# Value products in one run, rows scaled in the addition, attention's half first: one hybrid encoder layer on Trainium2

## The chip, the cores and the metric

The kernel runs on one core of one Trainium2 chip, in one launch. The metric is the device time in microseconds (us); lower is better. The times shown are medians of several runs, and beside them stands one execution taken with the hardware profiler. A core has five engines that run their own instruction streams: TensorE (PE, with its weight loads PEld), VectorE (DVE), ScalarE (ACT), GpSimd (POOL) and SyncE (SP), whose work here is the issue of DMAs.

## The reference

One layer of an encoder on x of 2048 rows by 1024 columns. Cut to what matters here:

```
proj = rms_norm(x, g_mix) @ w_in                      # q 8x64, k 2x64, v 2x64, u 512
attn = window_attention(rope(q), rope(k), v, sink)    # blocks of 128, window +-128, 512 wide
ys   = gelu(s5_bidirectional(u, ...))                 # state space, both directions, 512 wide
ys   = ys * sigmoid(ys @ w_glu)
mixed = concat([rms_norm(attn, g_attn), rms_norm(ys, g_ssm)])
x = x + mixed @ w_out
h = rms_norm(x, g_ffn)
up = depthwise_conv(h @ w_up, conv_w, conv_b)         # width 3
x = x + (silu(up[:, :2816]) * up[:, 2816:]) @ w_down
out = rms_norm(x, g_final)
```

A block of 128 queries sees up to three blocks of keys, its own and its two neighbours (the first and the last block see two). rms_norm divides every row by the root of the mean of its squares (plus a small constant) and multiplies each column by a gain.

## The kernel before

The kernel works in stages. First come the input projection and the tables of the state space part, then the state space part itself (s5), with the projections of q, k and v beside it. Then attention and the stage called join run side by side, and the feed-forward part (ffn) comes last. Products that need full float32 accuracy are made in three passes: a number is split into a high part that TensorE's faster float32 form (F32R) holds exactly and the rest, and `mm3` (lines 73 to 80) multiplies high by high, high by low and low by high into the same PSUM bank.

**Attention** (lines 478 to 630) is a generator. After its setup it takes five steps for each of 32 pairs (block b, key head kv), so ten steps a block. While it weighs the values of one pair it makes the logits and the softmax of the next:

1. `logits` of the next pair, query heads 0 and 1 (sp, line 556, with VectorE's masked maximum at line 557); for kv 0 the loads and splits of the next queries and keys.
2. `turn_p` for key tiles 0 and 1: four transposes each (ptp, line 579) and a copy by ScalarE (ph, line 581).
3. `logits`, heads 2 and 3; then `weigh` of key tile 0.
4. `turn_p` of key tile 2, `weigh` of key tile 1, and the `softmax` of the next pair (lines 559 to 573: exponentials on ScalarE, the division on VectorE).
5. `weigh` of key tile 2, which ends in ScalarE's copy of av into aT; for kv 0 `turn_q` and `turn_k`, transposes of the next queries and keys (ptq, ptk).

`weigh` (lines 584 to 591) multiplies one key tile's values (128 keys by 64) into two halves of the output's partitions, one matmul for each half. They are float32 and the trace has two records for each, so four for a call:

```
for o in (0, 1):
    nc.tensor.matmul(av[64 * o:64 * o + 64], vt[order[ki]][:, kv], ph4[:, o], start=ki == 0, ...)
```

**Join** (lines 632 to 811) is a generator too. For each block b it makes the output projection in two halves of 512 columns (po). Each half is five groups of matmuls, over parts 4 to 7 of the mixed row first (the state space half) and 0 to 3 (attention) after them. Behind each of the first four groups of a half it takes one item of a list called todo and yields; it also yields at the end of each half. That gives ten yields and eight slots to a block. The list has eight items:

- `gate(b + 2)`, three: loads y, transposes it (gpt, line 667), multiplies it by w_glu (pg), applies the gate, and scales the rows by their reciprocal root mean square rs (line 691).
- `turn(b - 1)`, two: transposes the normalised row block hx (gpt<-hx) and stores it, with sums and differences in the second four blocks of each half of the rows, as operands of the feed-forward part (lines 723 to 756). Some of these are made in hx itself and stored from there.
- `halves(b + 1)`, three: squares aT and sums it over the four parts (lines 707, 708); sums over the partitions with a matmul against ones (pr, line 711) and takes the power -1/2 on POOL (`rstd`, line 119), and transposes and splits y into parts 4 to 7; spreads that reciprocal over the columns with a matmul against the identity (pr, line 718), multiplies aT by it on VectorE (line 719) and splits it into parts 0 to 3.

At the end of a block the rows are x + po (line 794); they are stored, squared into hx (line 804), and hx becomes the normalised rows (line 807). There is one hx buffer.

**Order.** `build` advances attention by one step for each of join's yields in the steady part and by 1.5 before it. So a block of join goes with a block of attention, and join is at block b while attention works at b + 2. This is the program's order. The tile framework hands the instructions to the engines when the kernel is built, by a schedule of its own. In the trace PE's order in this stage is nearly the program's, with some instructions later than they are written, such as the transposes of keys among the po that follow. Each engine runs its own list in order and waits at an instruction until what it needs is there. PSUM here has three banks for join (R), one for av (psa), two for sp and two for transposes (pt).

Of the kernel before, what the change touches and what calls it, by code (L numbers as in the profile page):

```python
# [3 lines left out]

# [1 line left out]

# [17 lines left out]
NB = 16  # L24
# [5 lines left out]
EPS = 1e-6  # L30
# [25 lines left out]
class Net:  # L56
# [25 lines left out]
    def setup(self):  # L82
        nc, tc = self.nc, self.tc
        c = self.cpool = self.pool(self.ctx, "const")
        d = self.pool(self.ctx, "scratch", space=DRAM)
        self.ident = c.tile([128, 128], F32, name="ident")
        self.identr = c.tile([128, 128], F32R, name="identr")
        self.mhalf = c.tile([128, 1], F32, name="mhalf")
        nc.vector.memset(self.mhalf, -0.5)
        self.ones = c.tile([128, 1], F32, name="ones")  # L90
        nc.vector.memset(self.ones, 1.0)
        warm = c.tile([128, 1], F32, name="warm")
        nc.scalar.activation(warm, self.ones, AF.Copy)
        self.r16 = c.tile([128, 16, 2], F32, name="r16")
        self.rx = c.tile([128, NB], F32, name="rx")
        self.cw = c.tile([128, 2 * NF, 4], F32, name="cw")
        self.qkv_d = d.tile([L, 768], F32, name="qkv_d")
        self.u_d = d.tile([L, 512], F32, name="u_d")
        self.q_d = d.tile([T, 64, 128], F32, name="q_d")
        self.e_d = d.tile([16, 128, 2, 2, 128], F32, name="e_d")  # L100
        self.kp_d = d.tile([16, 2, 32, 2, 256], F32, name="kp_d")
        self.y_d = d.tile([L, 512], F32, name="y_d")
        self.x1_d = [d.tile([128, D], F32, name=f"x1_{t}") for t in range(NB)]
        self.bop_d = [{m: d.tile([128, 4, HALF], F32, name=f"bo{b}{m}") for m in BOP} for b in (0, 1)]
        self.act_d = [d.tile([2 * n, 128, L], F32, name=f"act{c}") for c, n in enumerate(DN)]
        self.wsum_d = [{m: d.tile([128, n, HALF], F32, name=f"ws{c}{m}") for m in ("t1", "t2", "t3", "t4")} for c, n in enumerate(DN)]
        self.gN = None
        self.st_f = ExitStack()
        self.left = False
# [368 lines left out]
    def attention(self):  # L478
        nc, tc, a = self.nc, self.tc, self.a
        V, S, G = nc.vector, nc.scalar, nc.gpsimd  # L480
        with ExitStack() as st:
# [117 lines left out]
            for n in range(2 * NB):  # L599
                b, kv = divmod(n, 2)  # L600
                nb, nkv = divmod(n + 1, 2)
                nk = len(window(b)[0])
                more, new = nb < NB, kv == 0 and b + 1 < NB
                if more:
                    logits(nb, nkv, (0, 1))
                if new:
                    qs = load_q(b + 1)
                    ks = load_kv(b + 2) if b + 2 < NB else None
                yield
                ph = [turn_p(b, kv, ki) for ki in (0, 1)]  # L610
                yield
                if more:
                    logits(nb, nkv, (2, 3))
                av = self.psa.tile([128, 512], F32, tag="pa", name=self.nm("av"))[:, 0:256]
                weigh(b, kv, av, 0, ph[0])
                yield
                if nk == 3:
                    ph.append(turn_p(b, kv, 2))
                weigh(b, kv, av, 1, ph[1])
                if more:  # L620
                    softmax(nb, nkv)
                yield
                if nk == 3:
                    weigh(b, kv, av, 2, ph[2])
                if new:
                    turn_q(b + 1, qs)
                    if ks is not None:
                        turn_k(b + 2, ks)
                del sms[b, kv]
                yield  # L630

    def join(self):
# [21 lines left out]
            return r  # L654

        def out_piece(n):
            k, c = (n + 4) % 8, n // 8
            r = p.tile([128, 512], F32, tag=("x1", "hx")[n % 3 == 2], name=self.nm("woraw"), bufs=2 - (n % 3 == 2))
            nc.sync.dma_start(r, a["w_out"][128 * k:128 * (k + 1), 512 * c:512 * c + 512])
            h, l, sc = wo[c][0][:, k], wo[c][1][:, k], gas[:, k:k + 1]  # L660
            S.activation(h, r, AF.Copy, scale=sc)
            V.scalar_tensor_tensor(l, r, sc, h.bitcast(F32), ALU.mult, ALU.subtract)
# [7 lines left out]
        def gate(b):  # L670
# [13 lines left out]

            S.activation(sg, pg, AF.Tanh, scale=0.5)
            V.scalar_tensor_tensor(y, sg, 1.0, y, ALU.add, ALU.mult)
            ssq = g.tile([128, 1], F32, tag="gssq", name=self.nm("gssq"))
            S.activation(sg, y, AF.Square, accum_out=ssq)
            rs = g.tile([128, 1], F32, tag="grs", name=self.nm("grs"))
            self.rstd(rs, ssq, 512, g, 4 * EPS)  # L690
            V.tensor_scalar(y, y, rs, None, ALU.mult)
            yield

        def halves(b):

            h = p.tile([128, 8, 128], F32R, tag="oh", name=self.nm("oh"))
            l = p.tile([128, 8, 128], F32R, tag="ol", name=self.nm("ol"))
            split[b] = h, l

            def part(src, k):  # L700
                S.activation(h[:, k:k + 4], src, AF.Copy)
# [4 lines left out]
            sr = p.tile([128, 128], F32, tag="sr", name=self.nm("sr"), bufs=1)  # L706
            S.activation(sq, aT, AF.Square)
            V.tensor_reduce(sr, sq.rearrange("p a q -> p q a"), axis=AX.X, op=ALU.add)
            yield
            pr = self.R.tile([128, 512], F32, tag="x", name=self.nm("pr"))  # L710
            nc.tensor.matmul(pr[:, 0:1], sr, self.ones[:, 0:1])
            ra = p.tile([128, 1], F32, tag="ra", name=self.nm("ra"))
            self.rstd(ra, pr[:, 0:1], 512, p)
            part(trans(ys.pop(b)), 4)
            yield

            pr = self.R.tile([128, 512], F32, tag="x", name=self.nm("pr"))
            nc.tensor.matmul(pr[:, 0:128], ra.to_broadcast([128, 128]), self.ident)
            V.tensor_tensor(aT, aT, bc(pr[:, 0:128], 1, 4), op=ALU.mult)
            part(aT, 0)  # L720
            yield

        def turn(b, hx):
# [48 lines left out]
            yield False  # L772
        hx = None
        for b in range(NB):
            h, l = split.pop(b)
            if b == NB - 2:
                gst.close()
            first = gate(b + 2) if b + 2 < NB else halves(b + 1) if b + 1 < NB else iter([None] * 4)
            todo = chain(first, turn(b - 1, hx) if b else (), halves(b + 1) if b + 2 < NB else ())
            rows = slice(128 * b, 128 * (b + 1))  # L780
            x1 = p.tile([128, D], F32, tag="x1", name=self.nm("x1"))
            nc.sync.dma_start(x1, a["x"][rows, :])
            for c in (0, 1):
                po = self.R.tile([128, 512], F32, tag="x", name=self.nm("po"))
                sl = slice(512 * c, 512 * c + 512)
                for n, ks in enumerate(((4, 5), (6, 7), (0, 1), (2,), (3,))):
                    self.mm3(po, [(h[:, k], l[:, k], wo[c][0][:, k], wo[c][1][:, k]) for k in ks], n == 0, n == 4)
                    for i in (next(late, None), next(late, None)):
                        if i is not None:
                            out_piece(i)  # L790
                    if n < 4:
                        next(todo, None)
                        yield True
                V.tensor_tensor(x1[:, sl], po, x1[:, sl], op=ALU.add)
                if c == 0:
                    if b == NB - 1:
                        wst.close()
# [579 lines left out]
```

## Time and profile before

| | |
|---|---|
| Median of three runs | 2161.92 us (2161.03 to 2167.24) |
| Profiled execution, its own time | 2166.09 us |
| Its span in the trace | 2164.3 us |
| PE busy | 2066.8 us (95%) |
| VectorE busy | 1696.6 us (78%) |
| ScalarE busy | 1054.1 us (49%) |
| POOL busy | 158.6 us (7%) |
| DMA moved | 320.14 MB |

Attention's value products run from 413.3 to 824.5 us in the trace, the output projection's matmuls from 450.5 to 859.5. Busy time is the time that an engine's instructions cover. Matmuls overlap: a matmul of 512 columns lasts about 0.39 us in the records, but the next begins before it ends. So the cost of a matmul in a row of matmuls is read from one start to the next. A line of the timeline gives start, length, engine, source line, operation, what is written from what, the shape, and how many equal instructions in a row it stands for. In brackets stands idle time before it, with what ended that. In a table of stretches the numbers behind an engine are its busy microseconds and, in brackets, its instructions; the granted clock of TensorE, the DMA engines' busy share and GB/s follow.

### The profile page before, as it was taken

The page shows a single profiled execution, that of the slowest core. Times are in us where ns is not written, and L with a number is a line of the kernel's source. Part 1 is how long each engine was busy: PE and PEld are TensorE (multiplying, and loading weights), DVE is VectorE, ACT ScalarE, POOL GpSimd, SP SyncE. Part 2 cuts the span into 40 slices and gives each one's busy share as a digit, 9 for nine tenths or more (in the row PEclk, how much of TensorE's full clock was granted, in tenths as well). Part 3 has the DMA queues.
Part 4 walks back from the last instruction along what each step waited for, and adds up shares of the span by engine and source line. Part 5 has one row for each costly group of instructions (what it writes and reads, how often), then busy time and mean ns, then how long its engine had stood idle before and what let it go on. Part 6 is the DMA issues. An engine that isn't in the chain of part 4 may idle for free.

```text
span 2164.3 us, 27908 instructions
## 1 busy us (share of the span) xinstructions
PE 2066.8 (95%) x10000; PEld 1667.8 (77%) x10000; DVE 1696.6 (78%) x3008; ACT 1054.1 (49%) x1847; POOL 158.6 (7%) x244
## 2 busy tenths in 40 slices
PE   7998889799999999999999999999999999998997
PEld 5787777567777777788888887888888787887886
DVE  8978888675566557788888898898988967756885
ACT  5524444776666654544444454544444634324332
POOL 0400000000000001000000000010100010000111
PEclk9999999899999999999999999999999999999999
DMA  8975655533244228522233363343432567856642
GB/s 280 343 196 153 193 168 168 165 103 93 76 130 122 77 80 258 170 88 82 96 107 125 117 208 109 122 164 119 149 138 86 163 151 196 203 110 182 183 158 88
DMA packets 204043, 320.14 MB, mean 148 GB/s; under 512 B 13312, under 2 KB 134656, under 8 KB 203904
## 3 DMA queue, kind: packets, MB, share of 16 engines
q1 hardware_dynamic: 182160, 245.41, 36.2%
q0 software_dynamic: 18304, 70.26, 11.1%
q10 hardware_dynamic: 3440, 2.69, 0.4%
q8 instruction: 78, 1.28, 0.2%
q14 instruction: 61, 0.50, 0.1%
HBM read 213.98 MB, written 104.33 MB: 147 GB/s over the span
## 4 chain that ended last, share of the span: by engine, by line
PE 68%; issue 10%; DMA 9%; DVE 9%; ACT 3%; POOL 1%; SPq 1%; ACTq 0%; POOLq 0%; DVEq 0%
PE py L1120 19%; PE pz L1120 12%; PE px L1120 12%; PE po L78 3%; PE av L589 2%; PE po L79 2%; PE po L80 2%; PE sp L556 2%; PE ptp L579 2%; DMA kp_d<-kk 2%; PE pp L80 1%; PE pp L79 1%; PE pp L78 1%; PE gpt L667 1%; DMA y_d<-yt 1%
## 5 line engine op out<-in xcount | busy, mean ns | idle before, releaser
L1120 PE MATMUL px<-b,g1h 128*128 128x512 f32 x1056 | 327.1, 391 | 6.1 <-ACT cu L1148 5.0
L1120 PEld LDWEIGHTS px<-b,g1h 128*128 128x128 f32 x1056 | 198.4, 188 | 49.4 <-ACT cu L1148 6.7
L1120 PE MATMUL px<-b,g1l 128*128 128x512 f32 x528 | 206.3, 391 | 1.1 <-DVE g1l L1043 0.9
L1120 PE MATMUL py<-bt,s2h 128*128 128x512 f32 x528 | 166.9, 398 | 4.6 <-ACT s2h L1042 4.6
L1120 PE MATMUL py<-bt,g2h 128*128 128x512 f32 x528 | 164.0, 391 | 3.7 <-DVE cu L1174 3.7
L1120 PE MATMUL py<-bt,s1h 128*128 128x512 f32 x528 | 162.9, 389 | 0.1
L1120 PE MATMUL pz<-bt,s1h 128*128 128x512 f32 x528 | 162.7, 389 | 0.0
L1120 PE MATMUL pz<-b,s4h 128*128 128x512 f32 x528 | 162.6, 389 | 0.0
L1042 ACT ACTIVATE s1h<-st 128x1024 fp32r<-128x1024 f32 (+1 forms) x67 | 69.4, 1036 | 120.8 <-PE py L1120 120.7
L1120 PEld LDWEIGHTS py<-bt,s2h 128*128 128x128 f32 x528 | 101.3, 192 | 26.8 <-ACT s2h L1042 5.8
L1120 PEld LDWEIGHTS py<-bt,g2h 128*128 128x128 f32 x528 | 99.1, 188 | 25.9 <-DVE cu L1174 4.1
L1120 PEld LDWEIGHTS px<-b,g1l 128*128 128x128 f32 x528 | 99.4, 188 | 22.9 <-DVE g1l L1043 2.2
L1120 PEld LDWEIGHTS py<-bt,s1h 128*128 128x128 f32 x528 | 99.1, 188 | 21.1 <-DVE bt L1008 0.5
L1120 PEld LDWEIGHTS pz<-b,s4h 128*128 128x128 f32 x528 | 99.1, 188 | 20.6
L1120 PEld LDWEIGHTS pz<-bt,s1h 128*128 128x128 f32 x528 | 99.1, 188 | 20.6
L1120 PE MATMUL py<-bt,s2l 128*128 128x512 f32 x264 | 105.8, 401 | 7.5 <-DVE s2l L1043 7.5
L1159 DVE TENSOR_TENSOR cu<-py,cu 128x512 f32<-128x512 f32 x68 | 46.9, 689 | 76.2 <-PE py L1120 76.2
L1042 ACT ACTIVATE g2h<-uraw 128x512 fp32r<-128x512 f32 x43 | 27.2, 632 | 156.3 <-PE py L1120 156.3
L1120 PE MATMUL py<-bt,g2l 128*128 128x512 f32 x264 | 102.9, 390 | 0.0
L1120 PE MATMUL py<-bt,s1l 128*128 128x512 f32 x264 | 102.7, 389 | 0.0
L1120 PE MATMUL pz<-bt,s1l 128*128 128x512 f32 x264 | 102.7, 389 | 0.0
L1120 PE MATMUL pz<-b,s4l 128*128 128x512 f32 x264 | 102.7, 389 | 0.0
(280 smaller groups left out, 5123.7 us busy)
## 6 DMA issues: line engine op xcount, KB each, us to landing
uraw<-in_w_up_dram SPq DMA_DIRECT2D x86, 512.0 KB
araw<-act SPq DMA_DIRECT2D x32, 512.0 KB
xr<-in_xT_dram SPq DMA_DIRECT2D x30, 512.0 KB
act<-cv POOLq DMA_DIRECT2D x22, 512.5 KB, 2.9
bsum<-in_w_down_dram SPq DMA_DIRECT2D x22, 512.0 KB
act<-cv POOLq DMA_DIRECT2D x22, 511.5 KB, 3.3
xn<-in_x_dram SPq DMA_DIRECT2D x16, 512.0 KB
qb<-q_d SPq DMA_DIRECT2D x64, 128.0 KB
```

The source lines that it names most:

```text
L78: nc.tensor.matmul(out, sh, mh, start=first and i == 0, stop=False)
L79: nc.tensor.matmul(out, sh, ml, start=False, stop=False)
L80: nc.tensor.matmul(out, sl, mh, start=False, stop=last and i == n - 1)
L556: nc.tensor.matmul(sp[:, :n], qTs[b][:, 4 * kv + j], kT[:, kv, i, slots], start=i == 0, stop=i == 1)
L579: nc.tensor.transpose(pt[:, 128 * j:128 * (j + 1)], sm[:, j, 128 * ki:128 * ki + 128], self.ident)
L589: nc.tensor.matmul(av[64 * o:64 * o + 64], vt[order[ki]][:, kv], ph4[:, o], start=ki == 0, stop=ki == len(order) - 1)
L667: nc.tensor.transpose(pt[:, 128 * k:128 * (k + 1)], src[:, 128 * k:128 * (k + 1)], self.ident)
L1042: S.activation(h[:, :c], src, AF.Copy)
L1120: nc.tensor.matmul(bank, x[:, k], o[:, y, k], start=first and k == 0 and i == 0, stop=k == kn - 1 and i == 2, skip_group_check=True)
L1159: V.tensor_tensor(old["vc"][:, lo], old["Y"], old["vc"][:, lo], op=ALU.add)
```

## The change

Three things change, all between attention and join.

First, the value products of one pair are issued together in its last step, six matmuls for three key tiles, and `turn_p` of tile 2 moves to step 3. `turn_q` and `turn_k` move to step 4, ahead of the softmax.

Second, the mixed rows are no longer scaled by attention's reciprocal ra ahead of the projection. The addition to x multiplies the whole projected row by ra. So that the state space half comes out right, y is multiplied by rs and by rv, the inverse of ra, in `halves` and not by rs in the gate. The matmul that spread ra and the multiplication of aT go.

Third, attention's parts 0 to 3 come first in each half of the projection, `out_piece` splits w_out in that order, and the list todo becomes gate, two steps of `halves`, `turn`, and the last step of `halves`.

```diff
@@ attention
                 if more:
                     logits(nb, nkv, (2, 3))
-                av = self.psa.tile([128, 512], F32, tag="pa", name=self.nm("av"))[:, 0:256]
-                weigh(b, kv, av, 0, ph[0])
-                yield
                 if nk == 3:
                     ph.append(turn_p(b, kv, 2))
-                weigh(b, kv, av, 1, ph[1])
-                if more:
-                    softmax(nb, nkv)
                 yield
-                if nk == 3:
-                    weigh(b, kv, av, 2, ph[2])
                 if new:
                     turn_q(b + 1, qs)
                     if ks is not None:
                         turn_k(b + 2, ks)
+                if more:
+                    softmax(nb, nkv)
+                yield
+                av = self.psa.tile([128, 512], F32, tag="pa", name=self.nm("av"))[:, 0:256]
+                for ki in range(nk):
+                    weigh(b, kv, av, ki, ph[ki])
                 del sms[b, kv]
                 yield
@@ gate
-            ssq = g.tile([128, 1], F32, tag="gssq", name=self.nm("gssq"))
+            r2 = g.tile([128, 2], F32, tag="grs", name=self.nm("grs"), bufs=3)
+            ssq, rs = r2[:, 0:1], r2[:, 1:2]
+            ys[b, "rs"] = rs
             S.activation(sg, y, AF.Square, accum_out=ssq)
-            rs = g.tile([128, 1], F32, tag="grs", name=self.nm("grs"))
             self.rstd(rs, ssq, 512, g, 4 * EPS)
-            V.tensor_scalar(y, y, rs, None, ALU.mult)
             yield
@@ halves
             V.tensor_reduce(sr, sq.rearrange("p a q -> p q a"), axis=AX.X, op=ALU.add)
+            part(aT, 0)
             yield
             pr = self.R.tile([128, 512], F32, tag="x", name=self.nm("pr"))
             nc.tensor.matmul(pr[:, 0:1], sr, self.ones[:, 0:1])
-            ra = p.tile([128, 1], F32, tag="ra", name=self.nm("ra"))
-            self.rstd(ra, pr[:, 0:1], 512, p)
-            part(trans(ys.pop(b)), 4)
-            yield
-
-            pr = self.R.tile([128, 512], F32, tag="x", name=self.nm("pr"))
-            nc.tensor.matmul(pr[:, 0:128], ra.to_broadcast([128, 128]), self.ident)
-            V.tensor_tensor(aT, aT, bc(pr[:, 0:128], 1, 4), op=ALU.mult)
-            part(aT, 0)
+            r3 = p.tile([128, 3], F32, tag="ra", name=self.nm("ra"))
+            va, rv, ra = (r3[:, i:i + 1] for i in range(3))
+            V.tensor_scalar(va, pr[:, 0:1], 1.0 / 512, EPS, ALU.mult, ALU.add)
+            nc.gpsimd.tensor_tensor(rv, va, self.phalf, op=ALU.pow)
+            nc.gpsimd.tensor_tensor(ra, va, self.mhalf, op=ALU.pow)
+            split[b] = h, l, ra
+            y = ys.pop(b)
+            V.tensor_scalar(y, y, ys.pop((b, "rs")), rv, ALU.mult, ALU.mult)
+            yield
+            part(trans(y), 4)
             yield
@@ join, the loop over blocks
-            first = gate(b + 2) if b + 2 < NB else halves(b + 1) if b + 1 < NB else iter([None] * 4)
-            todo = chain(first, turn(b - 1, hx) if b else (), halves(b + 1) if b + 2 < NB else ())
+            first = gate(b + 2) if b + 2 < NB else () if b + 1 < NB else iter([None] * 4)
+            two = halves(b + 1) if b + 1 < NB else iter(())
+            todo = chain(first, islice(two, 2), turn(b - 1, hx) if b else (), two)
...
-                for n, ks in enumerate(((4, 5), (6, 7), (0, 1), (2,), (3,))):
+                for n, ks in enumerate(((0, 1), (2, 3), (4, 5), (6,), (7,))):
...
-                V.tensor_tensor(x1[:, sl], po, x1[:, sl], op=ALU.add)
+                V.scalar_tensor_tensor(x1[:, sl], po, ra, x1[:, sl], ALU.mult, ALU.add)
```

`phalf` is a column of 0.5, made beside `mhalf`, and `out_piece` takes its part as n % 8 where it was (n + 4) % 8.

More of the change, by code (lines that the diff above doesn't have):

```diff
@@ L2 @@
 from contextlib import ExitStack
-from itertools import chain
+from itertools import chain, islice
 import numpy as np
@@ L89, in setup @@
         nc.vector.memset(self.mhalf, -0.5)
+        self.phalf = c.tile([128, 1], F32, name="phalf")
+        nc.vector.memset(self.phalf, 0.5)
         self.ones = c.tile([128, 1], F32, name="ones")
@@ L656, in out_piece @@
         def out_piece(n):
-            k, c = (n + 4) % 8, n // 8
+            k, c = n % 8, n // 8
             r = p.tile([128, 512], F32, tag=("x1", "hx")[n % 3 == 2], name=self.nm("woraw"), bufs=2 - (n % 3 == 2))
@@ L697, in halves @@
             l = p.tile([128, 8, 128], F32R, tag="ol", name=self.nm("ol"))
-            split[b] = h, l
             def part(src, k):
@@ L774, in join @@
         for b in range(NB):
-            h, l = split.pop(b)
+            h, l, ra = split.pop(b)
             if b == NB - 2:
                 gst.close()
-            first = gate(b + 2) if b + 2 < NB else halves(b + 1) if b + 1 < NB else iter([None] * 4)
-            todo = chain(first, turn(b - 1, hx) if b else (), halves(b + 1) if b + 2 < NB else ())
+            first = gate(b + 2) if b + 2 < NB else () if b + 1 < NB else iter([None] * 4)
+            two = halves(b + 1) if b + 1 < NB else iter(())
+            todo = chain(first, islice(two, 2), turn(b - 1, hx) if b else (), two)
             rows = slice(128 * b, 128 * (b + 1))
```

## The prediction

> **What bounds the kernel now.** I read the busy time by stretches first, to see which engine ends the stage that the change touches, and then the order of time of that engine alone, since its own records give the price of each step.
>
> ```profile
> span 2164.3 us, 27908 instructions
> core 0: us, PE busy (x) PEld busy (x) DVE busy (x) ACT busy (x) POOL busy (x), PEclk, DMA share, GB/s
> 440.00:825.00 385.00, 383.31 (x2171) 285.45 (x2170) 240.22 (x697) 242.09 (x606) 23.97 (x43) 1.00 0.32 99
> 825.00:880.00 55.00, 46.73 (x210) 36.16 (x210) 40.32 (x58) 24.99 (x37) 8.85 (x15) 0.97 0.89 277
> ```
>
> From 440 to 825 us, where attention and the output projection run side by side, PE is busy for 383.31 of 385 us at a granted clock of 1.00, VectorE for 240 and ScalarE for 242. So what PE no longer has to do there comes off the span, as long as the others stay ahead; they have some 140 us each to spare. From 825 on PE has 8 us of idle time and DMA is at 0.89: that tail I expect to move forward as a whole. Inside the stage these are PE's instructions in order of time, in one block (start, length; lengths overlap, so I price by starts):
>
> ```profile
> 561.19 0.86 PE L556 MATMUL sp<-kT,qT 128*128 128x384 f32 x4
> 561.98 0.65 PE L589 MATMUL av<-ph,kv 128*64 128x256 f32 x4
> 562.56 0.50 PE L78 MATMUL po<-wo0h,oh 128*128 128x512 f32 x1
> 562.90 0.39 PE L79 MATMUL po<-wo0l,oh 128*128 128x512 f32 x1
> 563.12 0.40 PE L80 MATMUL po<-wo0h,ol 128*128 128x512 f32 x1
> ...
> 563.83 0.39 PE L80 MATMUL po<-wo0h,ol 128*128 128x512 f32 x1
> 564.06 0.60 PE L667 MATMUL gpt<-ident,raw 128*128 128x128 f32 x4
> 564.49 0.60 PE L579 MATMUL ptp<-ident,sm 128*128 128x128 f32 x4
> 565.02 0.65 PE L589 MATMUL av<-ph,kv 128*64 128x256 f32 x4
> 565.61 0.50 PE L78 MATMUL po<-wo0h,oh 128*128 128x512 f32 x1
> 565.95 0.40 PE L79 MATMUL po<-wo0l,oh 128*128 128x512 f32 x1
> ...
> 568.28 0.40 PE L80 MATMUL pg<-gh,yl 128*128 128x512 f32 x1
> 568.61 0.65 PE L589 MATMUL av<-ph,kv 128*64 128x256 f32 x4
> 569.19 0.88 PE L540 MATMUL ptq<-identr,qs 128*128 128x128 f32 x8
> ...
> 575.03 1.04 PE L579 MATMUL ptp<-ident,sm 128*128 128x128 f32 x8
> ...
> 586.01 0.63 PE L667 MATMUL gpt<-ident,raw 128*128 128x128 f32 x4
> 586.40 0.48 PE L80 MATMUL po<-wo1h,ol 128*128 128x512 f32 x1
> 587.03 0.49 PE L718 MATMUL pr<-ident,ra 128*128 128x128 f32 x2 [0.15 <-POOL ra L123]
> 587.35 1.04 PE L579 MATMUL ptp<-ident,sm 128*128 128x128 f32 x8
> ...
> 589.71 0.65 PE L589 MATMUL av<-ph,kv 128*64 128x256 f32 x4
> ```
>
> The same av stands at 561.98 and 589.71, so one block takes 27.73 us, and each of its ten steps 2.77. Three po from 563.12 to 563.83 cost 0.71, 0.24 each; four transposes (564.06 to 564.49) cost 0.43. An av group is the two matmuls of one key tile, four records in all, and it costs far more than its place in the row of starts suggests. Between transposes and the second po after it, 564.49 to 565.95, lie 1.46 us; less 0.43 for the transposes and 0.24 for one po, 0.79 is left for the group. The group at 561.98 has the same distances behind it (0.58 to the first po, 0.34 to the second). The one at 568.61 has 0.91 from the pg ahead of it to the transposes behind, less 0.24: 0.67. Six groups are in a block: 5 x 0.79 + 0.67 = 4.62 us, the sixth kind (po on both sides, no row here) taken at 0.79 too.
>
> **Value products together.** The change issues the same matmuls, all key tiles of one block and key head in a row, so two groups of twelve records in place of six of four. What does a longer group cost? These rows are the second half of the group at 561.98, and a group elsewhere that also writes strips of columns:
>
> ```profile
> 562.24 0.39 PE L589 MATMUL av<-ph,kv 128*64 128x256 f32 x2
> 247.70 0.64 PE L862 MATMUL kp<-wc,Bs 128*32 128x256 f32 x8
> 248.15 0.22 PE L864 MATMUL kp<-wc,Bs 128*32 128x16 f32 x4
> ```
>
> The four av records run as two waves of two, the second 0.26 behind the first (562.24 less 561.98). So of 0.79 only two waves are work, and the rest is getting in and out: the 0.34 instead of 0.24 behind it, the 0.33 instead of 0.24 ahead of it, and 0.32 from the second wave to the po. A merged group pays that once and adds four waves. A wave costs between 0.225 (kp: 0.45 for two waves of 256 columns, one load in front included) and 0.26 (av). I take 0.225, since the added waves stand inside a run, as kp's second does, while av's 0.26 includes its first load. A group of three tiles then costs 0.79 + 4 x 0.225 = 1.69, two of them 3.38, and a block saves 1.24; at 0.26 it saves 0.96. Blocks 1 to 14 have three tiles: 14 x 1.24 = 17.4 (13.4 at 0.26). Block 15 has two: per key head 2 x 0.79 becomes 0.79 + 0.45, 0.34 saved, 0.7 in all. Block 0 lies ahead of the dense stretch and I count nothing for it (bounds 0 and 0.7). Sum 18.1, with 14.1 as the lower end.
>
> The rule that speaks against this: the Trainium skill, "TensorE: Matmul & The Clock Gate", in the section "The mechanism", says that a weight load overlaps running matmuls only where the row group differs, and all of these use all 128 rows. By it every added wave would show its load, and the 14.1 would be the sum; the kp rows, 0.225 with the load of the first wave in it, speak against it, with strips half as wide.
>
> **Rows scaled in the addition.** The matmul that spread ra over the columns (pr at L718) goes, and with it PE's wait for POOL. From the transposes at 586.01 to the next at 587.35 are 1.34 us; less 0.43 and one po, 0.24, that is 0.67 per block.
>
> ```profile
> L718 PE MATMUL pr<-ident,ra 128*128 128x128 f32 x28 | 6.5, 314 | 1.7 <-POOL ra L123 0.9
> ```
>
> There are two records to a block, 28 in the stretch, 14 blocks. Where nothing waits they may cost only their own mean, under 2 x 0.31. I take 0.67 for twelve blocks and 0.2 for the four at the two ends, 8.8 in all; bounds 6 and 10.7. On VectorE the multiplication of aT by pr goes, one of 512 columns a block, and the addition of x only gains a factor from a column; VectorE does not end the stage, so I count nothing (without that cover, some tenths of a microsecond a block, either way). POOL does one power more a block, with 24 us busy of 385. The multiplication of y by rs is moved from the gate into halves and now waits there for POOL's rv; behind it on VectorE stand the masked maxima of the logits and the addition of x, and PE waits for their PSUM banks. It waited for POOL's grs in the gate before, at the same length of chain, so this is an exchange, at nothing. PE's transposes of y come three steps after that, 8 us.
>
> **Attention's half first, and the order of steps.** The eight slots of a block (gate 3, turn 2, halves 3) become gate 3, halves 2, turn 2, halves 1. The scaled ssm half is ready at the last slot and used by the third group of the next block, the distance that the attention half had; no cost. turn is moved back, its first half by three steps and its second by two, and with it its transposes, its DMAs on SP and the time for which it holds hx, the one buffer that ScalarE's square at the end of the block overwrites:
>
> ```profile
> 608.56 0.52 SPq L729 DMA_DIRECT2D bo0t<-hx  x1
> ...
> 610.31 1.29 SPq L729 DMA_DIRECT2D bo0t<-hq  x2
> ...
> 614.14 1.24 SPq L733 DMA_DIRECT2D hq<-bo  x2
> 617.58 1.06 ACT L804 ACTIVATE hx<-x 128x1024 f32<-128x1024 f32 x1 [0.20 <-DVE x L794]
> ```
>
> hq's reload, which needs hq's store landed, was issued at 614.14, 3.8 after the store at 610.31, so a store lands within 3.8 of its issue. hx's at 608.56 was landed by 612.4, 5.2 ahead of the square. Moved by two steps of about 2.6 us that cover is just used up: no stall to a small one, in the eight blocks whose turn stores out of hx. I take 0 (bounds 0 and 1 us in each of eight blocks). Queued on SP behind the moved stores are the store of x1 and the load of x for the block after, used only at the end of a half block; they cost nothing while they land within that. The query turns now come ahead of the softmax in the program; that is a rival below.
>
> **Sum.** 18.1 + 8.8 = 26.9 us. The profiled execution took 2166.09 us, 1.8 more than its span, and would take 2139.2. It is 4.2 above the median of the runs shown, 2161.92; on that median the change gives 2135.0. A block should go from 27.73 to 27.73 - 1.24 - 0.67 = 25.8 us.
>
> **Rivals.** First, every added wave costs 0.26 because its load shows, as the page's rule has it: 14.1 + 8.8 = 22.9 saved, 2139.0. For it speaks the av row, against it kp's. Chance 0.12.
>
> Second, the change does not do what it says: the instructions are put in order by the framework's scheduler when the kernel is built, and it may set other work between the key tiles. Every group then still pays its way in and out, and only the 8.8 remain: 2153.1. In the stretch the order of PE's steps is nearly the program's, which speaks against it. Chance 0.08.
>
> Third, another wait takes part of the gain: the softmax. Its last multiplication and the transposes that need it are
>
> ```profile
> 568.27 1.41 DVE L573 TENSOR_SCALAR sm<-sm,den 128x384 f32<-128x384 f32 x4
> ```
>
> and the ptp at 575.03, so 5.35 us of cover. If ScalarE copied all query and key turns before the first exponential, the softmax would come some 3 us later (an estimate: twelve transposes at the 0.11 each of the four at 564.06, and the three copies behind them), and PE's half block is about 1 us shorter: 1.3 left. Should another 2 be lost, 0.7 us in each of 14 blocks goes, and 17 are saved: 2145. Chance 0.07.
>
> Fourth, slower: ScalarE's square waits for hx's store in the eight blocks, and with it everything queued behind on ScalarE, first the exponentials and the split of y, from which PE makes pg a step later. It decides from 26.9 / 8 = 3.4 us of PE's time in a block. A store that lands at 8 us rather than 3.8 would put the square 4 us late, which PE would feel in full only if nothing covered it; with 5 us lost in each it comes out at 2161.92 - 26.9 + 40 = 2175. In the dense stretch the DMA share is only 0.32, which speaks against it. Chance 0.05.
>
> **How the numbers follow.** The forecast has 0.68, the rivals 0.12, 0.08, 0.07 and 0.05. The predicted time is the forecast's, 2135. The range reaches down to 2128 (pr's upper bound of 1.9 more, block 0's 0.7, a wave at little over 0.2, and some microseconds of scatter, since the three runs span 6) and up to 2150, which takes in the first and the third rival and leaves out the second and the fourth, 0.13, with the ends of the rest. A measurement of this kernel can tell about 0.3% from no change, 6.5 us: all but the fourth rival save more. Some of the second and the fourth would end near zero. Faster 0.91, the same 0.04, slower 0.05.
>
> **What would show it.** Right: PE rows av x12 in the dense stretch, 1.69 from the instruction ahead to the second behind it less their own time; no pr at L718; the same av 25.8 us apart from block to block; PE still over 99% busy; the start of the px products about 27 us earlier. The first rival shows starts of av 0.26 apart throughout, the second av x4 rows, the third PE idle before ptp with a release by VectorE's sm, the fourth ScalarE idle before hx (L804) with a release by the store out of hx inside the stretch. Wrong outright: PE's share in the stretch falling under 97%, for then another engine ends the stage and PE's prices no longer add up.

## The result and the profile after

| kernel | median, us | runs | ratio to before, 95% interval |
|---|---|---|---|
| before, first set | 2161.48 (2160.84 to 2167.24) | 6 | |
| the change, first set | 2141.32 (2134.82 to 2142.98) | 6 | 0.9903 [0.9886, 0.9919] |
| the change, second set | 2134.67 (2132.6 to 2139.39) | 5 | 0.9882 [0.9857, 0.9908] |

The change is faster by 20.2 us in the first set and by 27.6 in the second (before there: 2162.25). The forecast was 2135.0, 26.9 saved, with a range of 2128 to 2150; both medians lie in it. The profiled execution took 2138.08 us, span 2136.3, against 2166.09 and 2164.3 before; the sum made on that execution's own time had given 2139.2.

The same view of busy time by stretches, on the changed kernel:

```profile
core 0: us, PE busy (x) PEld busy (x) DVE busy (x) ACT busy (x) POOL busy (x), PEclk, DMA share, GB/s
440.00:797.00 357.00, 356.11 (x2110) 285.11 (x2110) 231.15 (x678) 238.00 (x596) 34.27 (x59) 1.00 0.34 105
797.00:850.00 53.00, 43.92 (x195) 34.52 (x195) 37.41 (x52) 21.91 (x32) 9.42 (x16) 0.90 0.88 278
```

In the dense stage PE is still busy 99.8% of the time (356.11 of 357) at a clock of 1.00: it still bounds the stage, and prices read off PE's starts still add up. In the tail behind it the granted clock is 0.90, where it was 0.97. PE's rows in order of time, changed kernel:

```profile
556.65 0.40 PE L80 MATMUL pg<-gh,yl 128*128 128x512 f32 x1
556.98 1.51 PE L591 MATMUL av<-ph,kv 128*64 128x256 f32 x12
558.42 0.50 PE L78 MATMUL po<-wo0h,oh 128*128 128x512 f32 x1
...
568.44 0.60 PE L667 MATMUL gpt<-ident,hx 128*128 128x128 f32 x4
568.97 1.52 PE L591 MATMUL av<-ph,kv 128*64 128x256 f32 x12
570.42 0.50 PE L78 MATMUL po<-wo1h,oh 128*128 128x512 f32 x1
...
582.48 0.40 PE L80 MATMUL pg<-gh,yl 128*128 128x512 f32 x1
582.81 1.52 PE L591 MATMUL av<-ph,kv 128*64 128x256 f32 x12
584.25 0.50 PE L78 MATMUL po<-wo0h,oh 128*128 128x512 f32 x1
584.59 0.39 PE L79 MATMUL po<-wo0l,oh 128*128 128x512 f32 x1
```

The products stand in runs of twelve, two to a block, and the same run comes again after 25.83 us (556.98 to 582.81); 25.8 was forecast. From the pg at 582.48 to the second po behind the run are 2.11 us; less the two others at 0.235 each, the run costs 1.64, forecast 1.69. No row at the old L718 is left.

To see where the time went I cut each trace at the same five places: the first av, the normalised hx of block 0, that of block 12, the feed-forward part's first pz, and the end. Two profiles of each kernel show what is scatter:

| us | to first av | to hx, block 0 | to hx, block 12 | to first pz | to the end | span |
|---|---|---|---|---|---|---|
| before | 413.3 | 68.1 | 331.5 | 60.8 | 1290.6 | 2164.3 |
| before, second profile | 419.0 | 68.6 | 331.5 | 62.8 | 1282.7 | 2164.6 |
| the change | 412.9 | 62.8 | 308.6 | 65.0 | 1287.1 | 2136.3 |
| the change, second profile | 410.5 | 61.6 | 309.1 | 66.8 | 1284.9 | 2132.9 |

The twelve blocks repeat to 0.5 us and give 22.6. The way into the stage gives 6.2 (mean of two against mean of two), and the tail takes 4.1 back. The first and the last column differ by up to 8 us between two profiles of the same kernel: nothing can be read from them, and they carry the scatter of the times.

The largest single loss there has a place. This is the tail's longest wait of PE in the changed kernel, with the rows on ScalarE and VectorE that lead to it:

```profile
807.39 0.40 PE L80 MATMUL po<-wo0h,ol 128*128 128x512 f32 x1
812.92 1.94 PE L667 MATMUL gpt<-ident,hx 128*128 128x128 f32 x8 [5.12 <-DVE hx L809]
814.51 0.78 PE L78 MATMUL po<-wo1h,oh 128*128 128x512 f32 x1
```

```profile
807.09 1.06 ACT L806 ACTIVATE hx<-x 128x1024 f32<-128x1024 f32 x1 [3.09 <-DMA bo1t<-hx]
808.05 0.19 ACT L806 ACTIVATION_READ_ACCUMULATOR hx<-x 128x1 f32 x1
808.14 1.04 ACT L1009 ACTIVATE b<-braw 128x1024 fp32r<-128x1024 f32 x1
```

```profile
808.27 0.15 DVE L124 TENSOR_SCALAR rsv<-ossq 128x1 f32<-128x1 f32 x1 [2.37 <-ACT hx L806]
...
809.22 1.22 DVE L1010 TENSOR_TENSOR b<-braw,b 128x1024 fp32r<-128x1024 f32 x1 [0.73 <-ACT b L1009]
810.36 1.22 DVE L1010 TENSOR_TENSOR bt<-braw,bt 128x1024 fp32r<-128x1024 f32 x1
811.49 1.27 DVE L809 SCALAR_TENSOR_TENSOR hx<-x,r,gfr 128x1024 f32<-128x1024 f32 x1
```

PE stands for 5.12 us for hx of block 13. Read backwards: VectorE makes hx at 811.49, behind two splits of feed-forward operands (L1010, 2.3 us); the sum of squares it starts from came from ScalarE's square at 807.09; and that had waited 3.09 us for a store out of the one hx buffer. That is the fourth rival's mechanism, where the steps are short and the DMA share near 1, and nowhere in the dense stage. But it is not new in the tail. ScalarE's squares of the last blocks waited for stores of the turned rows in the kernel before too, for longer in sum, only at blocks 14 and 15 and not at 13 (total, times, longest; the first line is before, the second the change):

```profile
ACT hx L804 <- DMA bo1t<-hx: 8.5, 2, 5.5
ACT hx L806 <- DMA bo1t<-hx: 4.9, 2, 3.1
```

So the store explains where PE waits, and not by itself why the tail is longer. Before, PE did not wait for hx of block 13 at all, and its one wait for an hx, that of block 14, was 1.07 us:

```profile
856.54 1.09 PE L667 MATMUL gpt<-ident,hx 128*128 128x128 f32 x8 [1.07 <-DVE hx L807]
857.39 0.48 PE L80 MATMUL po<-wo1h,ol 128*128 128x512 f32 x1
```

The wait of 5.12 us also costs more than its length. Eight transposes took 1.59 us behind it (812.92 to 814.51) and 0.85 before. The changed kernel's stretches around it:

```profile
807.40:812.90 5.50, 0.39 (x2) 0.01 (x1) 3.90 (x6) 2.73 (x4) 3.33 (x5) 0.75 1.02 305
807.80:810.10 2.30, 0.00 (x0) 0.00 (x0) 1.10 (x3) 2.30 (x4) 1.53 (x3) 1.00 1.13 359
812.90:816.80 3.90, 3.88 (x14) 3.42 (x15) 1.57 (x3) 1.67 (x3) 0.00 (x0) 0.50 1.07 365
816.80:821.00 4.20, 4.20 (x22) 3.48 (x21) 4.20 (x7) 2.43 (x4) 0.53 (x1) 0.98 0.90 301
```

For 3.9 us behind the wait the granted clock is 0.50, so some 1.9 us more are lost. The Trainium skill, "TensorE: Matmul & The Clock Gate", section "What's actually happening", has it that the clock falls to a half after an idle window of about 3.4 us and comes back after as long a busy one; for the way back this trace roughly agrees (about 4 us of matmuls at a half). For the fall it does not: the clock is still 1.00 at 810.1 and, with a mean of 0.75 over the 5.5 us, down from about 810.2 on, some 2.4 us after PE's last matmul ended. Shorter waits were enough elsewhere: 2.22 us with the products alone and 2.86 with two hx buffers (both kernels below), while 2.39 us in the rest alone, 2.46 with the old order in the last three blocks, and the 1.07 above were followed by no fall. The stretch behind the wait of 2.86:

```profile
812.10:815.40 3.30, 2.89 (x11) 2.73 (x12) 1.43 (x3) 0.63 (x1) 0.53 (x1) 0.50 0.98 381
```

### The profile page after: what moved, and what is told of

The parts are those of the page before. It is cut to its first block, busy times and chain, and to the rows that moved or that the text cites. A ratio compares the mean times of both kernels' runs of the same rounds, so it can differ in the third digit from the quotient of the medians.

```text
span 2136.3 us, 27808 instructions
## 1 busy us (share of the span) xinstructions
PE 2045.6 (96%) x9968; PEld 1673.0 (78%) x9968; DVE 1688.4 (79%) x2993; ACT 1053.4 (49%) x1847; POOL 173.8 (8%) x260
## 4 chain that ended last, share of the span: by engine, by line
PE 65%; issue 12%; DMA 10%; DVE 8%; ACT 2%; POOL 1%; SPq 1%; POOLq 0%; ACTq 0%; DVEq 0%
PE py L1122 18%; PE pz L1122 11%; PE px L1122 11%; DMA kp_d<-kk 3%; PE po L78 3%; PE po L80 2%; PE po L79 2%; PE av L591 2%; PE sp L558 2%; PE ptp L581 2%; PE pp L80 2%; PE pp L78 2%; PE pp L79 2%; PE gpt L667 1%; DMA braw<-in_w_down_dram 1%
## 5 line engine op out<-in xcount | busy, mean ns | idle before, releaser
L1044 ACT ACTIVATE g2h<-uraw 128x512 fp32r<-128x512 f32 x43 | 27.2, 632 | 154.1 <-PE py L1122 154.1
```

The lines of the kernel that those rows point to most:

```text
L1044: S.activation(h[:, :c], src, AF.Copy)
```

## The experiments

**One part alone.** First the order of the value products alone (the first part of the diff), then everything else alone.

```diff
@@ attention (products alone; join as before)
-                weigh(b, kv, av, 0, ph[0])
...
+                for ki in range(nk):
+                    weigh(b, kv, av, ki, ph[ki])
@@ join (the rest alone; attention as before)
-                V.tensor_tensor(x1[:, sl], po, x1[:, sl], op=ALU.add)
+                V.scalar_tensor_tensor(x1[:, sl], po, ra, x1[:, sl], ALU.mult, ALU.add)
```

> The value products in one run alone, everything else as before: attention's five steps as in the change, scaling and order of the mixed parts as before. If PE's prices are what counts, a block of the dense stretch goes from 27.73 us to about 26.5 (two runs of 12 records at 1.65 in place of 4.62 us), the time falls by some 17 us, and the pr at L718 still shows its 0.67 a block. If the gain of the change came from elsewhere (the later place of the softmax, the wait for POOL), the block stays within 0.3 of 27.73.

> The scaling in the addition, attention's half first and the new order of the slots, with attention's steps and its value products as before. By PE's prices a block takes about 27.1 us (27.73 less 0.67) and the time falls by about 9 us, less whatever the tail loses. If the two parts are not independent, so that the scaling pays only once PE has less to do, the block stays at 27.73; if the moved turn stalls the square into hx, PE shows idle time in the second four blocks of each eight.

> The change itself, unchanged, for a second profile and a second set of times. In the first profile the span fell by 28.0 us while the median of the times fell by 20.2. If that difference is scatter from execution to execution, this profile shows the same dense block (25.84 us) and the same start of pz, and a difference elsewhere, of a size with the scatter of the times (some 8 us among six runs). If the times hold something that the profile does not, the median falls by about 20 again and the span by 28.

| us | median | ratio | twelve blocks | saved per block | tail |
|---|---|---|---|---|---|
| products alone | 2145.04 | 0.9929 [0.9903, 0.9954] | 313.3 | 1.52 | 67.3 |
| the rest alone | 2159.88 | 0.9996 [0.9981, 1.001] | 323.6 | 0.66 | 70.2 |
| the change | 2134.67 | 0.9882 [0.9857, 0.9908] | 309.1 | 1.87 | 66.8 |

The products bring nearly all of the time. The rest alone does shorten each block by the forecast 0.66, but 7.9 us in the twelve blocks are followed by a tail longer by 7.4 to 9.4, and nothing is left. On top of the products it brings 0.35 a block only. The two savings are not additive, and the next experiment shows most of the reason.

**The new order of the eight slots alone**, in the kernel before, with pr and the scaling kept:

```diff
-            first = gate(b + 2) if b + 2 < NB else halves(b + 1) if b + 1 < NB else iter([None] * 4)
-            todo = chain(first, turn(b - 1, hx) if b else (), halves(b + 1) if b + 2 < NB else ())
+            first = gate(b + 2) if b + 2 < NB else () if b + 1 < NB else iter([None] * 4)
+            two = halves(b + 1) if b + 1 < NB else iter(())
+            todo = chain(first, islice(two, 2), turn(b - 1, hx) if b else (), two)
```

> The kernel before with nothing but the new order of the slots (gate, two steps of halves, turn, the last step of halves); scaling, value products and order of the mixed parts as before, so the matmul that spreads ra is still there, but three steps behind the power it waits for. If the 0.67 us of that matmul are half wait, a block takes about 27.4 us here and PE no longer waits for POOL; if it is the matmul itself, 27.7. If the moved turn is what costs the tail, hx of block 13 is late here too (over 25 us behind that of block 12, 23.9 before) and the start of pz gains nothing or loses some microseconds.

2161.77 us, ratio 1.0012 [0.9992, 1.0032]; 327.1 us for the twelve blocks, 0.37 less each, and a tail of 67.3. PE's rows around pr there:

```profile
589.49 0.40 PE L80 MATMUL po<-wo1h,ol 128*128 128x512 f32 x1
589.73 0.39 PE L718 MATMUL pr<-ident,ra 128*128 128x128 f32 x2
589.95 1.04 PE L579 MATMUL ptp<-ident,sm 128*128 128x128 f32 x8
```

Here pr costs 0.22 (589.73 to 589.95) and waits for nothing. In the kernel before it cost 0.67 at its place, one po behind transposes and ahead of ptp. So 0.45 of the 0.67 belonged to that place (the wait for POOL, listed as 0.15, among it), and two different shifts of the order take it away; 0.22 is the matmul itself. The kernel with the products alone has the same 0.23 at its pr (578.19 to 578.42): it had taken that part of the saving already. That leaves 0.22 for the rest, where 0.35 was measured. The difference is a wait that only the products alone have: in four blocks in the middle of the stage PE waits 0.17 or 0.18 us for VectorE's sum sr at the matmul against ones (L709 there), and these last 26.4 to 26.6 us, where four of the blocks without it last 26.0, 0.2 above the change.

**The third key tile a step later**, in the changed kernel: two groups a block become five (8 + 4 records for one head, 6 + 2 around the key transposes and 4 for the other).

```diff
+                av = self.psa.tile([128, 512], F32, tag="pa", name=self.nm("av"))[:, 0:256]
+                for ki in range(nk - 1):
+                    weigh(b, kv, av, ki, ph[ki])
...
-                for ki in range(nk):
-                    weigh(b, kv, av, ki, ph[ki])
+                weigh(b, kv, av, nk - 1, ph[nk - 1])
```

> The whole change, but the third key tile's value products one step behind the first two, so two groups of 8 and 4 records in place of one of 12. If the way in and out of a group is what was saved, 0.34 us come back for every pair, and a block takes 25.84 + 0.7 = 26.5 us. If the length of the run does not matter (the gain came from the order of the steps), it stays at 25.84.

```profile
568.42 1.08 PE L591 MATMUL av<-ph,kv 128*64 128x256 f32 x8
...
571.46 0.65 PE L591 MATMUL av<-ph,kv 128*64 128x256 f32 x4
...
581.05 1.08 PE L591 MATMUL av<-ph,kv 128*64 128x256 f32 x6
582.06 0.54 PE L513 MATMUL ptk<-identr,ks 128*128 128x128 f32 x4
582.53 0.65 PE L591 MATMUL av<-ph,kv 128*64 128x256 f32 x2
...
586.09 0.65 PE L591 MATMUL av<-ph,kv 128*64 128x256 f32 x4
```

2149.63 us, one run; a block takes 26.84 us, 1.0 more than the change, for three groups more. The number of matmuls is the same, and PE lists no wait in the stage, so what is paid is the way into and out of a group: 0.33 us each.

**Both heads in one run of 24.** If 0.33 goes with each group, one group less in a block should save it again. A first attempt held the first head's turned weights back and wrote both heads' products one after the other, with one copy for each (it also had the tail's order of the kernel before, below).

```diff
+                if kv == 0:
+                    held = ph
+                else:
+                    av = self.psa.tile([128, 512], F32, tag="pa", name=self.nm("av"))
+                    for i, hs in enumerate((held, ph)):
+                        for ki in range(nk):
+                            weigh(b, i, av[:, 256 * i:256 * i + 256], ki, hs[ki])
```

> The change with the tail as before, and the value products of both key heads of a block in one run of 24 records, at the end of the second head's steps (six ph buffers, one qs and one qt). One way in and out less: 0.34 us a block, so 25.5 in the dense stretch, and some 4 us less in all than with the tail alone, if nothing else becomes late. If aT is then late for halves, or the single buffers of the queries are, PE shows idle time before sp or the projections and the gain is gone.

```profile
750.64 1.51 PE L591 MATMUL av<-ph,kv 128*64 128x256 f32 x12
752.09 0.50 PE L78 MATMUL po<-wo1h,oh 128*128 128x512 f32 x1
752.42 0.39 PE L79 MATMUL po<-wo1l,oh 128*128 128x512 f32 x1
752.65 0.40 PE L80 MATMUL po<-wo1h,ol 128*128 128x512 f32 x1
752.98 1.52 PE L591 MATMUL av<-ph,kv 128*64 128x256 f32 x12
```

```profile
PEld av L591 <- ACT aT L593: 4.4, 12, 0.4
```

2141.6 us, ratio 0.9904 [0.988, 0.9929], 25.8 a block. It does not do what it says: ScalarE's copy of the first head's half stood between the two runs, the second run waited for it (4.4 us in twelve waits), and three po were set in between. So it says nothing on the price. The second attempt has one copy of both halves behind the last product, the same buffers as the first, and the tail's order of the change:

```diff
+                    S.activation(self.aT[b], av.rearrange("p (j q) -> p j q", j=4), AF.Copy)
```

> The changed kernel with the value products of both key heads written as one run of 24 records into one tile, with one copy of it, after the second head's weights are turned. Theory A (a change between the two shapes of records costs 0.33 us for each group, as the kernel that held the third key tile back showed): one group less in each block, 25.83 - 0.33 = 25.5 us a block, 4 to 5 us in all: 2131 to 2132 us. Theory B (the two heads' groups already stand next to each other's work so that nothing is left to gain, or the scheduler splits the run of 24 again): 25.8 us a block and 2134 to 2138. Theory C (the output product that follows has to wait for the one copy, which is now at the end of the block): over 26 us a block.

```profile
718.50 2.81 PE L591 MATMUL av<-ph,kv 128*64 128x256 f32 x24
721.25 0.50 PE L78 MATMUL po<-wo1h,oh 128*128 128x512 f32 x1
...
743.96 2.81 PE L591 MATMUL av<-ph,kv 128*64 128x256 f32 x24
746.71 0.50 PE L78 MATMUL po<-wo1h,oh 128*128 128x512 f32 x1
```

A block takes 25.46 us (718.50 to 743.96), 0.37 less than the change, and the twelve blocks 304.0. 2133.47 us, ratio 0.9866 [0.9844, 0.9888], span 2127.0: the fastest of the kernels here by its trace. Its interval overlaps those of the change: the stage is shown to be faster than in the change, the whole time is not.

**The tail: where turn stands.** My first theory of the lost 4 us was that the last blocks' turn, moved back, is what comes too late. One kernel sets halves ahead of turn in block 14, another takes the order of before in the last three blocks.

```diff
-            todo = chain(first, islice(two, 2), turn(b - 1, hx) if b else (), two)
+            todo = chain(first, islice(two, 3 if b == NB - 2 else 2), turn(b - 1, hx) if b else (), two)
```

```diff
-            todo = chain(first, islice(two, 2), turn(b - 1, hx) if b else (), two)
+            back = turn(b - 1, hx) if b else ()
+            todo = chain(first, islice(two, 2), back, two) if b < NB - 3 else chain(first, back, two) if b == NB - 3 else chain(two, first, back)
```

> The whole change, but in block 14 all three steps of halves stand ahead of turn(13), as before. Theory: the 5.1 us in which PE waited at the transposes of hx in the tail come from that turn being one slot earlier than hx is ready; with it back, the wait falls to about 1 us as before, the feed-forward part starts some 4 us earlier, and the time falls by 3 to 4 us against the change. Rival: hx is late in any case and the feed-forward part waits for other things (loads, the last turn); then the wait moves and the start of pz stays within 1 us.

> The whole change with the order of the slots of before in the last three blocks of join (turn(12) directly behind the gate in block 13, all of halves ahead of turn(13) in block 14). The run with only block 14 put back did not shorten the tail, so that theory fell. New theory: what is late is hx of block 13, because turn(12), moved back, stores out of the one hx buffer 3.1 us too late for ScalarE's square; then ScalarE shows no wait for that store here, hx of block 13 comes 3 to 4 us earlier (at most 25 us behind that of block 12, not 27), and the time falls by 2 to 4 us against the change. Rival: VectorE's and ScalarE's splits of the feed-forward operands, queued ahead of hx, set the tail; then hx of block 13 stays 27 us behind.

2136.69 us (0.9891 [0.9862, 0.9919]) and 2139.14 (0.9898 [0.9875, 0.9922]); tails of 67.3 and 67.1 us. Both theories fall. With only block 14 put back, PE waits 6.46 us there for y's scaled rows (raw) in place of hx. With the order of before in the last three blocks, hx of block 13 comes 23.7 us behind that of block 12 (27.2 in the change), but the loss has moved behind it, where PE now waits five times, for three things (total, times, longest):

```profile
PE gpt L667 <- DVE ol L701: 3.1, 1, 3.1
PE gpt L667 <- DVE raw L719: 2.7, 2, 2.5
PE gpt L667 <- DVE hx L810: 2.4, 2, 2.1
```

**The tail: the hx buffer, the opening, and the kernel before once more.**

```diff
@@ two hx buffers
-            hx = p.tile([128, D], F32, tag="hx", name=self.nm("hx"), bufs=1)
+            hx = p.tile([128, D], F32, tag="hx", name=self.nm("hx"), bufs=2)
@@ opening held back
-            elif n > 10 * NB - 20:
+            elif n > 10 * NB + 99:
...
-        for _ in early:
+        for _ in net.ffn_open():
```

> The changed kernel with two buffers for hx (and one each for the turned and scaled q, to make room). Theory A (the single hx buffer, whose store must leave before the next normalisation's square may write, stretches the tail): the wait of ScalarE's square of block 13 for the store of block 12 (3.09 us in the changed kernel) is gone, the normalisation of block 13 stands 3 to 4 us earlier, and hx of block 12 to the first pz falls from 65 to 67 us to 61 to 63; about 2132 us where the change gives 2136. Theory B (what is late in the tail is late for several reasons, the queues of POOL and VectorE behind it among them): hx of block 13 moves by at most 1 us or the loss turns up in another block, and the time stays within 2 us of the change's. The dense stage stays at 25.8 us a block under both, unless one buffer for q makes its turn wait.

> The changed kernel with the opening of the feed-forward part (its first weight pieces, their splits on VectorE and POOL's loads) held back until the last block of this part has ended. Theory A (the opening's loads and splits, which stand ahead of hx in the queues of VectorE and POOL, make hx of block 13 late): PE's wait of 5.12 us for it falls below 1.5 us and hx of block 12 to the last output product (po) shortens by 3 to 4 us; the first pz, however, then waits for the weights that were held back, by an estimate 5 to 15 us, so the time as a whole is longer. Theory B (the tail is late without the opening too): the wait for hx of block 13 stays at 4 to 5 us.

> The kernel before, profiled a second time. In its first profile block 12's hx stood at 812.9 us and the feed-forward part's first pz at 873.7 us, a tail of 60.8 us; in every other kernel so far the tail is 64.9 to 70.2 us. Theory A (the tail of the changed order is longer because the order is changed): the second profile shows 60 to 62 us again. Theory B (60.8 was a lucky execution, and the tail scatters by several microseconds in any kernel): 64 us or more, and then the changed order's tail has cost nothing that can be told from scatter. The dense stage should repeat to 0.05 us a block (27.7) under both.

With two hx buffers no square waits for a store, and hx of block 13 comes 24.95 us behind block 12. Yet the tail is 70.6 us and the median 2145.09 (0.9915 [0.9892, 0.9938]): the loss moved again, as the second theory had it, and grew, which that theory had not. ScalarE's and PE's rows there:

```profile
814.77 1.06 ACT L1009 ACTIVATE bt<-braw 128x1024 fp32r<-128x1024 f32 x1 [4.87 <-DMA braw<-bo0t]
815.73 0.58 ACT L738 ACTIVATE hT<-gpt 128x512 f32<-128x512 f32 x1
```

```profile
812.51 1.94 PE L667 MATMUL gpt<-ident,hx 128*128 128x128 f32 x8 [2.86 <-DVE hx L809]
856.77 1.22 PE L1122 MATMUL pz<-bt,s1h 128*128 128x512 f32 x2 [7.41 <-ACT hT L749]
```

Now ScalarE stands for 4.87 us at the split of a feed-forward operand that is still being loaded, and the copies of the turned rows queue behind it; in the end the first pz waits 7.41 us for such a copy. The kernel meant to hold the opening back did not: its splits at L1010 start at 804.2 us, where those of the change start at 804.7, and PE's wait for hx of block 13 is 6.07 us. It took 2136.3 us in one run and tells only that the wait repeats. Whether the opening causes it was not tested. The second profile of the kernel before took 2166.37 us; its tail is 62.8 us, between what the two theories there had asked for, and its wait for hx 0.9. So the tail of before scatters by 2 us, and both its values lie below the shortest of the other kernels, 65.0.

## Why the prediction was right, and where it was not

**The dense stage was right by its steps.** 1.24 for the products and 0.67 for pr were to come off a block, 22.9 in twelve blocks; the traces have 22.6. The difference between the change (25.83) and the rest alone (27.07) is 1.24. Each added wave costs 0.215 (the six waves of the run at 582.81 start 0, 0.27, 0.48, 0.70, 0.91 and 1.13 us behind its start), where 0.225 was taken. Only the second wave shows 0.27, as av's second had shown 0.26 before. So the first rival falls, and with it the use made here of the rule in "TensorE: Matmul & The Clock Gate", "The mechanism" (the Trainium skill): the added waves do not cost 0.26, although all strips use the same rows. How much of a wave is its load these rows do not tell.

**The price of pr was right as a sum and partly wrong as to what it is.** 0.67 goes, but 0.45 of that belonged to where pr stood, not to the matmul. The prediction read the waits in the 0.67 as part of pr's removal; the new order of the slots takes that part away by itself.

**Work taken at nothing was nothing in the dense stage.** PE has no wait that the profile lists between 476 and 784 us. ScalarE's square there waits 2.9 us in all, for VectorE's x and for no store:

```profile
L806 ACT ACTIVATE hx<-x 128x1024 f32<-128x1024 f32 x13 | 13.8, 1061 | 2.9 <-DVE x L796 2.9
```

**The way in was undersized.** Between the first av and hx of block 0 lie the products of blocks 0 to 2. By the same prices, 16 groups at 0.79 less two runs of eight (1.24) and four of twelve (1.69) save 3.4 us, and two pr less 1.3: 4.7, where the prediction had two blocks of products in there and nothing for block 0. Measured were 6.2. The rest may be a wait of PE's key transposes for ScalarE's copy of qT, 2.2 and 3.0 us in the two profiles of before, which those of the change do not list. The mean granted clock in this stretch differs too, 0.89 and 0.91 before and 0.96 and 0.94 in the change. None of this was tested, so how much of the 6.2 the prices explain stays open.

**The step that failed is "that tail I expect to move forward as a whole".** It moved, but grew by 4.1 us. PE's listed waits in it add up to 9.0 and 10.1 us in the two profiles of the change and to 6.6 and 7.0 before, and the mean granted clock in it is 0.92 in both against 0.97 and 0.95. The new wait is that for hx of block 13, 5.1 and 5.5 us, with about 1.9 lost at half clock behind it; some of that is made good later. One sign in the prediction shows the changed order there: the px products were to start 27 us earlier. Their bulk does start 25.4 earlier (859.78 to 834.38), but before, a first pair stood at 837.47, ahead of block 13's transposes, and in the change none does. What the fourth rival priced for the dense stretch happened in the tail only, where the kernel before has such waits too. The size of the loss is shown, and the chain that leads to the longest wait in the change. The cause of the longer tail stays open, since no kernel made to remove one link of that chain removed the loss: in every kernel with a changed order, one whose blocks are only 0.4 us shorter among them, the tail is 65 to 71 us, against 60.8 and 62.8, and what PE waits for there differs from one to the next.

**The scatter** is as large as the missed terms, and the closeness of 2134.67 to the forecast is in part luck. The stages as traced give 22.6 + 6.2 - 4.1 = 24.7 us where 26.9 were forecast, so a way in that gave more and a tail that gave less partly cancel; the same changed kernel saved 20.2 us in one set of runs and 27.6 in the other, and the profiles show such differences ahead of the first av and behind the first pz, where the change does nothing of weight.

## What to carry to other kernels

On a TensorE that bounds its stage, count groups and not only matmuls: each separate group of matmuls with 128*64 weights, set among matmuls with 128*128 weights, cost a third of a microsecond here, so equal shapes belong together, and a copy between two runs is enough to split them. Check with the trace that they really stand together. A saving in a dense stage must still pass through the stage behind it: read that one's waits as a schedule of its own, since it can take back a seventh of the gain (4.1 of 28.8 us), or all of it where only 8 us were won. A shorter tail at one wait is not a shorter tail: three changes each removed or moved a wait here and none shortened the tail.

## What the hardware showed that was not expected

- A wait of 5.12 us on TensorE was followed by 3.9 us at a granted clock of 0.50, and so costs some 1.9 us more than it shows. Waits of 2.22 and 2.86 us were followed by about 3 us at 0.50, others of 2.39 and 2.46 by none: between these lengths the wait alone does not tell.
- A float32 run of strips settles at 0.215 us for a wave of two records of 256 columns, and a run of 24 records took 2.75 us to the next po where two of twelve take 1.44 and 1.45 each.
- The same matmul of 128 columns (pr, two records) cost 0.22 us in a row of po and ptp, and 0.67 at its place in the kernel before, also between a po and a ptp but closely behind transposes, with a listed wait of only 0.15.
